# A 64-byte pad ahead of the weight ring's second pool: matmul operands at one address modulo 512

## Chip, cores and metric

One core of one Trainium2 chip. The metric is the device time of one execution in microseconds (us); the kernel before was run three times. SBUF, the core's working memory, has 128 partitions, and an address below is a byte offset in a partition. The engines are named as in the profile: PE is TensorE's matmuls, PEld its weight loads, DVE VectorE, ACT ScalarE, POOL GpSimd, SP SyncE.

## What is computed

A two-layer encoder trunk over 256 frames of width 2048, in fp32. Layer 0 mixes with RWKV-7 and Mamba-2 heads behind one input projection, layer 1 with chunked attention; each ends with a SwiGLU block. What matters here is that nearly all work is eight dense products of a 256-row activation with a large weight:

```python
p = h @ w_in                                          # layer 0: 2048 -> 6144 (padded)
y = jnp.concatenate([y_a, y_b], axis=-1) @ w_out      # 2048 -> 2048
f = (jax.nn.silu(h @ w_gate) * (h @ w_up)) @ w_down   # both layers: 2048 -> 2 x 5632 -> 2048
q, k, v = jnp.split(h @ w_qkv, 3, axis=-1)            # layer 1: 2048 -> 6144
out = attention(q, k, v) @ w_out                      # 2048 -> 2048
```

## The kernel before

**The products.** Each weight is cut into blocks of 128 rows by 512 columns. `stream` (L218) brings two blocks with one 512 KB DMA into a `raw` buffer (four of them) and splits each into two fp32r tiles: ACT copies `raw` to `hi` (L235), DVE writes the remainder to `lo` (L236). The activation is split in the same way into a high and a low part (`sh` and `sl`, in the feed-forward's second product `hh` and `hl`, in attention's output product `oh` and `ol`). `mm_chunk` (L240) then makes one 512-column chunk of the output from 16 weight blocks (44 in the feed-forward's second product), and issues for each block six matmuls: for both halves t of the 256 rows,

```python
pe.matmul(o, lhsT=xh, rhs=h_[:, :width], ...)   # L255  high x hi
pe.matmul(o, lhsT=xh, rhs=l_[:, :width], ...)   # L256  high x lo
pe.matmul(o, lhsT=xl, rhs=h_[:, :width], ...)   # L257  low x hi
```

The **stationary** operand (`lhsT`) is a 128x128 slice of the activation, loaded into the array ahead of its matmul; the **moving** operand (`rhs`) is the weight tile, 512 columns that are streamed past it. Below, "a block" is one weight block and its six matmuls, from one L255 with t = 0 to the next.

**The order.** In the program's order the products are w_in (192 blocks), w_oab (64), then w_gu (352: gate and up) and w_dn (176) of layer 0, w_qkv (192), w_oc (64), and w_gu (352) and w_dn (176) of layer 1. Among their matmuls stand the rest of PE's work, in plain fp32: transposes against an identity matrix in `cc`, attention's scores and values, the two recurrences of layer 0. The feed-forward transposes its hidden tile `sg` (`ht`, L376) as soon as DVE has made it (L367); attention transposes each head's probabilities (`pt`, L905) behind a softmax on DVE and ACT.

**Where the tiles lie.** Pools lie one behind another in SBUF, in the order in which they are opened. `cst` holds constants, `cc` among them; `wpool` the `raw` buffers and five `hi` and five `lo` tiles; `S` the activations of 4 KB (`sh` and `sl` of every product but w_dn and w_oc); `sm` small statistics. Behind `sm` come first the pools of layer 0's mixer (R, R1, R2, M). When that mixer is done they are given up, and in their place open `wx` (L848), with four more `hi` and four more `lo` tiles, and behind it in turn the pools of the feed-forward (`sg`, `hh`, `hl`) and of attention (`oh`, `ol` among them).

From then on `stream` takes its tiles from a ring of nine turns:

```python
ring[:] = [wpool, wx, wpool, wx, wpool, wx, wpool, wx, wpool]     # L849
wp = ring[turn[0] % len(ring)]; turn[0] += 1                      # L230, once a block
```

The turn counter has run since the first block of w_in, so the pool of each block can be worked out: block 5 of chunk 9 of layer 0's w_gu has turn 192 + 64 + 9 x 16 + 5 = 405, a multiple of nine, so that it and the block ahead of it (turn 404, remainder 8) both lie in `wpool`. In w_in all blocks lie in `wpool`.

The addresses at which the built program puts the operands of the products, modulo 512:

```
operand                                          pool     address mod 512
moving, from wpool (all of w_in, 5 turns of 9)   wpool    192
moving, from wx (4 turns of 9)                   wx       128
stationary of w_in, w_oab, w_gu, w_qkv           S        192
stationary of w_dn (hh, hl), w_oc (oh, ol)       ff, O    128
```

A stationary slice starts a multiple of 512 bytes into its tile, so these remainders hold for all slices.

Of the kernel before, what the change touches and what calls it, by code (L numbers as in the profile page):

```python
# [9 lines left out]
F32 = mybir.dt.float32  # L10
# [6 lines left out]
P = 128  # L17
# [124 lines left out]
def encoder_body(ctx: ExitStack, tc: tile.TileContext, A):  # L142
# [7 lines left out]
    turn = [0]  # L150
    S = ctx.enter_context(tc.tile_pool(name="S", bufs=12))
    sm = ctx.enter_context(tc.tile_pool(name="sm", bufs=2))
    pmm = ctx.enter_context(tc.tile_pool(name="pmm", bufs=4, space=PSUM))
    pra = ctx.enter_context(tc.tile_pool(name="pra", bufs=2, space=PSUM))
    psa = ctx.enter_context(tc.tile_pool(name="psa", bufs=2, space=PSUM))
# [790 lines left out]
```

## Time and profile before

| | |
|---|---|
| three runs, median (lowest to highest) | 2434.82 us (2432.24 to 2435.89) |
| the profiled execution: its own time, its span | 2435.0 us, 2433.2 us |
| PE busy, PEld busy | 2400.9 us (99%), 1937.6 us (80%) |
| DVE busy, ACT busy, POOL busy | 1425.6 us (59%), 1267.9 us (52%), 33.2 us (1%) |
[...]
| HBM traffic | 425 MB read, 176 GB/s over the span |

The span runs from the first to the last instruction. [...]

### The profile page before, as it was taken

To read this page: it belongs to the slowest core of one execution; us is meant where nothing else is said; L and a number is where in the kernel's file an instruction comes from. 1 tells how busy PE (TensorE), PEld (TensorE's weight loads), DVE (VectorE), ACT (ScalarE), POOL (GpSimd) and SP (SyncE) were. 2 spreads that over 40 slices of the span, in tenths; PEclk is the share of its full clock that TensorE was granted. 3 is DMA by queue.
4 is the path that set the end of the run, shared out by engine and by line. 5 is a ranking of instruction groups with operands and counts; after the bars stand their busy time and mean duration, and the time that the engine had idled before them with its cause. 6 is when DMAs were issued, how large, how long until landed. Compare 5 with 4: busy or idle time off the path is not lost.

```text
span 2433.2 us, 31534 instructions
## 1 busy us (share of the span) xinstructions
PE 2400.9 (99%) x11374; PEld 1937.6 (80%) x11374; DVE 1425.6 (59%) x2364; ACT 1267.9 (52%) x2256; POOL 33.2 (1%) x60
## 2 busy tenths in 40 slices
PE   8999999999999999999999999999999999999998
PEld 7777778778888888888887878787888888888887
DVE  5865967665555555555556555556555555555554
ACT  6646545656444444444446555556544544444443
POOL 0000000000000000000000000000000000000000
PEclk9999989999999999999999999999999999999999
DMA  6433424656666666666665655566666666666664
GB/s 228 142 110 116 136 86 130 205 175 198 185 184 187 189 183 188 185 189 194 195 206 175 181 175 161 169 188 177 190 188 183 189 182 189 185 187 189 198 194 144
DMA packets 119357, 429.17 MB, mean 176 GB/s; under 512 B 13408, under 2 KB 13664, under 8 KB 119200
## 3 DMA queue, kind: packets, MB, share of 16 engines
q1 hardware_dynamic: 115424, 415.46, 56.1%
q0 software_dynamic: 2400, 9.18, 1.4%
q10 hardware_dynamic: 1376, 2.52, 0.3%
q8 instruction: 89, 1.46, 0.2%
q14 instruction: 68, 0.56, 0.1%
HBM read 425.01 MB, written 2.10 MB: 176 GB/s over the span
## 4 chain that ended last, share of the span: by engine, by line
PE 93%; DVE 3%; ACT 1%; DMA 1%; issue 1%; SPq 0%; POOL 0%; DVEq 0%; ACTq 0%; POOLq 0%
PE mm_w_gu L256 13%; PE mm_w_gu L255 13%; PE mm_w_gu L257 13%; PE mm_w_dn L255 7%; PE mm_w_dn L257 7%; PE mm_w_dn L256 7%; PE mm_w_qkv L255 4%; PE mm_w_qkv L256 4%; PE mm_w_qkv L257 4%; PE mm_w_in L257 3%; PE mm_w_in L256 2%; PE mm_w_in L255 2%; PE mm_w_oc L255 1%; PE mm_w_oab L256 1%; PE mm_w_oc L257 1%; PE mm_w_oab L255 1%
## 5 line engine op out<-in xcount | busy, mean ns | idle before, releaser
L236 DVE TENSOR_TENSOR lo_w_gu<-raw_w_gu,hi_w_gu 128x512 fp32r<-128x512 f32 x704 | 486.3, 692 | 434.2 <-ACT hi_w_gu L235 432.8
L235 ACT CAST hi_w_gu<-raw_w_gu 128x512 fp32r<-128x512 f32 x704 | 436.3, 621 | 474.8 <-PE mm_w_gu L257 420.4
L256 PE MATMUL mm_w_gu<-lo_w_gu,sh_f 128*128 128x512 f32 x1408 | 556.6, 396 | 0.0
L255 PE MATMUL mm_w_gu<-hi_w_gu,sh_f 128*128 128x512 f32 x1408 | 555.4, 394 | 0.6 <-ACT sh_f L294 0.5
L257 PE MATMUL mm_w_gu<-hi_w_gu,sl_f 128*128 128x512 f32 x1408 | 551.6, 392 | 0.0
L236 DVE TENSOR_TENSOR lo_w_dn<-raw_w_dn,hi_w_dn 128x512 fp32r<-128x512 f32 x352 | 243.1, 692 | 230.1 <-ACT hi_w_dn L235 230.1
L235 ACT CAST hi_w_dn<-raw_w_dn 128x512 fp32r<-128x512 f32 x352 | 217.8, 620 | 258.5 <-PE mm_w_dn L257 213.7
L255 PEld LDWEIGHTS mm_w_gu<-hi_w_gu,sh_f 128*128 128x128 f32 x1408 | 263.9, 187 | 65.4 <-ACT sh_f L294 3.4
L257 PEld LDWEIGHTS mm_w_gu<-hi_w_gu,sl_f 128*128 128x128 f32 x1408 | 264.2, 188 | 60.8 <-DVE sl_f L295 1.2
L256 PEld LDWEIGHTS mm_w_gu<-lo_w_gu,sh_f 128*128 128x128 f32 x1408 | 264.0, 188 | 58.0 <-DVE lo_w_gu L236 0.3
L255 PE MATMUL mm_w_dn<-hi_w_dn,hh 128*128 128x512 f32 x704 | 278.8, 396 | 0.0
L257 PE MATMUL mm_w_dn<-hi_w_dn,hl 128*128 128x512 f32 x704 | 277.0, 394 | 0.0
L256 PE MATMUL mm_w_dn<-lo_w_dn,hh 128*128 128x512 f32 x704 | 275.3, 391 | 0.0
L236 DVE TENSOR_TENSOR lo_w_qkv<-raw_w_qkv,hi_w_qkv 128x512 fp32r<-128x512 f32 x192 | 132.3, 691 | 101.1 <-ACT hi_w_qkv L235 101.1
L235 ACT CAST hi_w_qkv<-raw_w_qkv 128x512 fp32r<-128x512 f32 x192 | 118.6, 619 | 105.2 <-PE mm_w_qkv L257 94.2
L236 DVE TENSOR_TENSOR lo_w_in<-raw_w_in,hi_w_in 128x512 fp32r<-128x512 f32 x184 | 124.8, 688 | 56.3 <-ACT hi_w_in L235 54.9
L257 PEld LDWEIGHTS mm_w_dn<-hi_w_dn,hl 128*128 128x128 f32 x704 | 132.3, 188 | 31.6
L256 PEld LDWEIGHTS mm_w_dn<-lo_w_dn,hh 128*128 128x128 f32 x704 | 132.3, 188 | 30.4
L255 PE MATMUL mm_w_in<-hi_w_in,sh_in 128*128 128x512 f32 (+1 forms) x384 | 154.6, 403 | 1.4 <-ACT hi_w_in L235 1.4
L256 PE MATMUL mm_w_qkv<-lo_w_qkv,sh_qkv 128*128 128x512 f32 x384 | 155.5, 405 | 0.0
L257 PE MATMUL mm_w_in<-hi_w_in,sl_in 128*128 128x512 f32 (+1 forms) x384 | 155.4, 405 | 0.0
L255 PEld LDWEIGHTS mm_w_dn<-hi_w_dn,hh 128*128 128x128 f32 x704 | 132.0, 188 | 28.7
(343 smaller groups left out, 2854.5 us busy)
## 6 DMA issues: line engine op xcount, KB each, us to landing
raw_w_gu<-in_w_gu SPq DMA_DIRECT2D x352, 512.0 KB, 3.6
raw_w_dn<-in_w_dn SPq DMA_DIRECT2D x176, 512.0 KB, 4.1
raw_w_qkv<-in_w_qkv SPq DMA_DIRECT2D x96, 512.0 KB, 3.6
raw_w_in<-in_w_in SPq DMA_DIRECT2D x92, 512.0 KB, 3.6
raw_w_oab<-in_w_oab SPq DMA_DIRECT2D x32, 512.0 KB, 4.3
raw_w_oc<-in_w_oc SPq DMA_DIRECT2D x32, 512.0 KB, 3.9
bias<-in_bias POOLq DMA_DIRECT2D x4, 768.0 KB, 7.4
x_in<-in_x SPq DMA_DIRECT2D x4, 512.0 KB, 10.4
```

What stands on the lines that cost most here:

```text
L235: act.copy(hi, raw[:, h, :])
L236: dve.tensor_tensor(lo, raw[:, h, :], hi.bitcast(F32), op=ALU.subtract)
L255: pe.matmul(o, lhsT=xh, rhs=h_[:, :width], start=k_ == 0, stop=False)
L256: pe.matmul(o, lhsT=xh, rhs=l_[:, :width], start=False, stop=False)
L257: pe.matmul(o, lhsT=xl, rhs=h_[:, :width], start=False, stop=k_ == nk - 1)
```

## The change

A tile of 16 floats, 64 bytes in each partition, is allocated in `sm` and used by nothing:

```diff
     sm = ctx.enter_context(tc.tile_pool(name="sm", bufs=2))
+
+    pad_sm = sm.tile([P, 16], F32, tag="pad", name="pad_sm", bufs=1)
     pmm = ctx.enter_context(tc.tile_pool(name="pmm", bufs=4, space=PSUM))
```

In the built program every address behind it is 64 bytes higher, and each engine has the same instructions in the same order with the same waits. `cst`, `wpool` and `S` lie ahead of `sm` and stay. Some start addresses, before and after:

```
                              before            after
wpool hi, first tile          38080 (192)       38080 (192)      in brackets: mod 512
S, first tile                 58560 (192)       58560 (192)
wx hi, first tile            112768 (128)      112832 (192)
sg, first tile               129152 (128)      129216 (192)
hh, first tile               137344 (128)      137408 (192)
oh, first tile               186496 (128)      186560 (192)
cc                            16512 (128)       16512 (128)
```

Modulo 2048 the `wpool` tiles stand at 1216 in both kernels, those of `wx` at 128 before and 192 after.

## Rows read from the trace of the kernel before

**Rows 1.** The page: span, and busy us of each engine (share) xinstructions.
```profile
span 2433.2 us, 31534 instructions
PE 2400.9 (99%) x11374; PEld 1937.6 (80%) x11374; DVE 1425.6 (59%) x2364; ACT 1267.9 (52%) x2256; POOL 33.2 (1%) x60
```
**Rows 2.** The page: the chain that ended last, by engine.
```profile
PE 93%; DVE 3%; ACT 1%; DMA 1%; issue 1%; SPq 0%; POOL 0%; DVEq 0%; ACTq 0%; POOLq 0%
```
**Rows 3.** Groups of PE by line and shape: count | busy us, mean ns | idle us before.
```profile
L255 PE MATMUL mm_w_gu<-hi_w_gu,sh_f 128*128 128x512 f32 x1408 | 555.4, 394 | 0.6 <-ACT sh_f L294 0.5
...
L376 PE MATMUL ht<-cc,sg 128*128 128x128 f32 x176 | 26.6, 273 | 0.0
...
L305 PE MATMUL pn_f<-cc,m_o 128*128 128x128 f32 x32 | 4.8, 272 | 0.0
```
**Rows 4.** Timeline of PE in w_in: start us, duration us, engine, line, tiles.
```profile
231.88 0.39 PE L255 MATMUL mm_w_in<-hi_w_in,sh_in 128*128 128x512 f32 x1
...
250.70 0.39 PE L257 MATMUL mm_w_in<-hi_w_in,sl_in 128*128 128x512 f32 x1
```
**Rows 5.** Timeline of PE in w_gu: first matmul of some blocks.
```profile
733.26 0.39 PE L255 MATMUL mm_w_gu<-hi_w_gu,sh_f 128*128 128x512 f32 x1
...
742.96 0.39 PE L255 MATMUL mm_w_gu<-hi_w_gu,sh_f 128*128 128x512 f32 x1
...
744.36 0.39 PE L255 MATMUL mm_w_gu<-hi_w_gu,sh_f 128*128 128x512 f32 x1
...
745.74 0.39 PE L255 MATMUL mm_w_gu<-hi_w_gu,sh_f 128*128 128x512 f32 x1
...
747.10 0.39 PE L255 MATMUL mm_w_gu<-hi_w_gu,sh_f 128*128 128x512 f32 x1
```
**Rows 6.** Timeline of PE in w_dn: first matmul of some blocks.
```profile
1101.40 0.39 PE L255 MATMUL mm_w_dn<-hi_w_dn,hh 128*128 128x512 f32 x1
...
1112.48 0.40 PE L255 MATMUL mm_w_dn<-hi_w_dn,hh 128*128 128x512 f32 x1
...
1113.87 0.39 PE L255 MATMUL mm_w_dn<-hi_w_dn,hh 128*128 128x512 f32 x1
...
1115.24 0.40 PE L255 MATMUL mm_w_dn<-hi_w_dn,hh 128*128 128x512 f32 x1
...
1116.63 0.40 PE L255 MATMUL mm_w_dn<-hi_w_dn,hh 128*128 128x512 f32 x1
```
**Rows 7.** Stretches: us, busy PE, PEld, DVE, ACT, POOL, clock, DMA share, GB/s.
```profile
231.88:250.70 18.82, 18.82 (x85) 15.58 (x83) 14.24 (x23) 17.41 (x29) 0.17 (x1) 1.00 0.52 153
733.26:758.22 24.96, 24.96 (x109) 20.24 (x108) 12.47 (x19) 12.46 (x20) 0.00 (x0) 1.00 0.64 190
1101.40:1126.34 24.94, 24.94 (x110) 20.28 (x109) 12.47 (x19) 11.16 (x18) 0.00 (x0) 1.00 0.65 209
```
**Rows 8.** Timeline of PE in w_in, behind transposes of the mixer.
```profile
125.92 0.40 PE L256 MATMUL mm_w_in<-lo_w_in,sh_in 128*128 128x512 f32 x1
...
128.69 0.39 PE L256 MATMUL mm_w_in<-lo_w_in,sh_in 128*128 128x512 f32 x1
```
**Rows 9.** Timeline of PE in attention: a head's transposes, the matmul ahead of each.
```profile
1348.89 0.40 PE L255 MATMUL mm_w_qkv<-hi_w_qkv,sh_qkv 128*128 128x512 f32 x1
1349.21 0.61 PE L905 MATMUL pt<-cc,s 128*128 128x128 f32 x3
...
1354.25 0.40 PE L255 MATMUL mm_w_qkv<-hi_w_qkv,sh_qkv 128*128 128x512 f32 x1
1354.53 0.61 PE L905 MATMUL pt<-cc,s 128*128 128x128 f32 x3
```
**Rows 10.** What reads tile sg: who ended the idle time (us, times).
```profile
  DVE sg L367: 8.9, 44
```
**Rows 11.** Lines 235 and 236: duration ns min/median/max, first and last start us.
```profile
L235 ACT CAST hi_w_gu<-raw_w_gu x704: 602/621/642, 518.6 to 2168.3; 128x512 fp32r<-128x512 f32 x176
L236 DVE TENSOR_TENSOR lo_w_gu<-raw_w_gu,hi_w_gu x704: 671/693/695, 519.2 to 2169.0; 128x512 fp32r<-128x512 f32 x176
```

## The prediction

> **What bounds the kernel now.** I read the page's list of engines first: PE is busy 2400.9 of 2433.2 us, DVE 1425.6 and ACT 1267.9 [rows 1]. The chain of waits says the same of the end: 93% of it is PE [rows 2]. So the time is the number of matmuls times the pace at which they follow each other, and anything that changes the pace by one per cent moves the end by one per cent. The groups of PE [rows 3] give the counts: 1408 L255 matmuls in w_gu are two (one for each half t) of each of 704 blocks, as the program has it. All products together have 1568 blocks of six matmuls, 9408 in all.
>
> The pace is in the timelines, from start to start. In the stretch of w_in [rows 4] 84 matmuls stand without a break; the last begins 250.70 - 231.88 = 18.82 us after the first, over 83 steps, which is 0.2267 us a step and **1.360 us for a block of six**. Here moving and stationary operands both lie at 192 modulo 512. In w_gu [rows 5] the ring shows. The block from 742.96 has its weights in `wx`, at 128, against a stationary 192, and takes 1.40 us. The next, from 744.36, is back in `wpool`, 192 against 192, and takes 1.38. The one from 745.74 is the second `wpool` block in a row (turn 405), and takes 1.36 (to 747.10), the pace of w_in. The shape and the engine's clock are the same in all three. What differs is where the weights lie, and where those of the block before lay. A whole cycle of nine blocks, from 733.26 to 745.74, takes 12.48 us: 1.387 a block. In w_dn [rows 6], where the stationary lies at 128, the cycle from 1101.40 to 1113.87 takes 12.47 us, 1.386 a block; its blocks take 1.39 (from 1112.48, `wpool` after `wx`), 1.37 (from 1113.87, second `wpool` block) and 1.39 (from 1115.24, `wx`, 128 against 128).
>
> Could another load than the addresses make w_in faster? The stretches [rows 7] show the full clock, 1.00, in all three. DMA moves 153 GB/s in that of w_in and 190 and 209 in the others, which would be a candidate; but the fast block of w_gu stands in the midst of the heavier traffic and has the same 1.36.
>
> **The change part by part.** The tile itself costs nothing: no instruction writes or reads it, and no order or wait changes. What moves is every address behind `sm`.
>
> *w_gu, w_qkv, w_oab* (704 + 192 + 64 = 960 blocks). Four blocks of nine move from 128 to 192, so that all have the pairing 192 against 192 and none follows another. I take the pace of w_in: 1.387 - 1.360 = 0.0267 us a block, 25.6 us. The bounds: nothing gained where a block stays at 1.40 and 1.38; 25.6 where all settle.
>
> *w_dn, w_oc* (352 + 64 = 416 blocks). Here the stationary moves from 128 to 192 too, and the pairing becomes the same one. From 1.3855 (12.47 / 9) to 1.360 is 0.0255 us a block, 10.6 us. The trace never shows these stationary pools (`ff`, `O`) at 192; the nearest rows are those of `S` at 192, which I take, with 0 as the other end.
>
> *w_in* (192 blocks) stays: its operands lie ahead of the pad. Together 36.2 us, if every block had the settled pace.
>
> *Breaks.* Behind other PE work the stream needs about ten steps to settle, at equal addresses too: behind transposes in w_in twelve steps take 128.69 - 125.92 = 2.77 us instead of 12 x 0.2267 = 2.72 [rows 8], which is 0.05 lost. Outside w_in some 100 such breaks stand in the program (44 groups of `ht`, 44 in attention, the rest in the norms), many with fewer steps behind them. I count 0.03 us each, between 0 (a break with nothing to settle) and the row's 0.05: 3.0 us are not gained, with 0 and 5 as ends.
>
> *Waits that now come later.* In attention a head's transposes `pt` already wait for the softmax: the matmul ahead starts 0.32 and 0.28 us before them, instead of 0.23 [rows 9], and from one to the next pass 5.32 us, a time that DVE and ACT set. PE has some 20 matmuls of the product between (5.32 us less about 0.9 for the head's own small ones, at 0.23) and gains 20 x 0.0045 = 0.09 us there, which turns into waiting. Twelve of the sixteen heads follow another one closely: 1.1 us lost. The weight loads of `ht` wait for DVE 44 times, 8.9 us in all [rows 10], in the shadow of the matmul that still runs. PE comes there some five matmuls after the one that released DVE, so at most 5 x 0.0045 = 0.02 us earlier: between 0 and 1.0 us lost, and I take 0.5.
>
> *The weights' supply* holds. A block costs ACT 0.62 and DVE 0.69 us [rows 11] of now 1.36, and the DVE group's narrow spread (671 to 695 ns, over `lo` tiles at 192 and at 128) speaks against a price of the address there. The *transposes* lose the equality with `cc` at 128 that `ht` has now; `pn_f`, whose tile at 192 is unequal to it, takes 272 ns against 273 [rows 3], so I take nothing, with 176 x 1 ns = 0.2 us as the other end.
>
> The sum: 36.2 - 3.0 - 1.1 - 0.5 = 31.6 us. Against the profiled execution's own 2435.0 us that is 2403.4; it stands 0.2 above the median of the three runs, so that I forecast **2403 us**.
>
> [...]
>
> **The rivals.**
>
> *Only part of it counts (2423 us).* The rule could be one of equality modulo 2048, not 512: `wpool` stands at 1216 there, `wx` at 192 after the change. Then the `wx` blocks keep their 1.40 and only the four `wpool` blocks behind them go from 1.38 to 1.36: 4 x 0.02 = 0.08 of a cycle's 12.48 us, times 1376 / 9 = 153 cycles, 12 us. Against it: stationary slices step by 512 bytes through all four remainders modulo 2048, and the 84 matmuls in w_in [rows 4] keep one pace through all of them.
>
> *No change (2435 us).* The slow blocks may be slow since the ring alternates between two far pools, or for where `wx` lies, whatever the remainder. For it: in the trace before, `wx` and 128 always go together in w_gu. Against it: in w_dn, in the same ring, `wx` and `wpool` blocks both take 1.39, so that it isn't the pool alone.
>
> *Slower (2455 us).* Equal addresses may be the bad case and w_in an exception. For it: in w_dn the block at equal addresses, 128 against 128, takes 1.39 and the unequal one from 1113.87 takes 1.37. If every block came to the 1.40 that the slowest ones take, 960 x 0.013 + 416 x 0.0145 = 18.5 us would be added, nearly 2454, with the waits behind it 2455. It decides where a run of equal blocks settles: above 1.387 us the kernel is slower, below it faster. Against it: such runs are what w_in is made of, and they settle at 1.360; the 128 block in w_dn always follows one at 192 and is never settled.
>
> *More than counted (2398 us):* no breaks and waits lost, the full 36.2.
>
> **How the numbers follow.** The forecast has 0.84, since the pairing that it leads to stands in the trace at its pace, under the same clock and the same traffic. "More" has 0.02, "part" 0.06, "no change" 0.05, "slower" 0.03. What a measurement of this kernel can tell from no change is about 0.2%, 5 us: faster 0.84 + 0.02 + 0.06 = 0.92, same 0.05, slower 0.03. The range goes down to 2395, which is the full 36.2 with the 3 us by which the shown runs scatter. Upward it goes to 2412: 9 us above the forecast, about what w_dn and w_oc bring, should they stay as they are. That covers the first and the last of the cases and leaves some 0.15 outside.
>
> **What would show it.** In the changed kernel's timeline each block of w_gu, w_dn, w_qkv and w_oc, `wx` or `wpool`, should take 1.36 us, but for some ten matmuls behind each break, and a cycle of nine 12.24. PE's busy time should fall by about 32 us and its share stay at 99%; w_in's timeline, ACT's 0.62 and DVE's 0.69 should stay. `pt` should start some 0.4 us behind the matmul ahead. Blocks of 1.40 in the places of `wx`, alternating with 1.36, would prove "part" right; 1.40, 1.38 and 1.36 in the old order "no change"; 1.387 or more throughout the last rival. A w_dn that settles elsewhere than w_gu would mean that the stationary pool counts by itself.

## The result and the profile after

Four runs of the changed kernel took 2402.06 us in the median (2400.69 to 2404.57), beside 2433.74 us of the kernel before: a ratio of 0.987, 95% interval 0.9853 to 0.9887. The forecast was 2403 us.

The page of the changed kernel, span, PE and chain, to be held against [rows 1, 2]:

```profile
span 2399.9 us, 31534 instructions
PE 2367.5 (99%) x11374; PEld 1937.3 (81%) x11374; DVE 1424.7 (59%) x2364; ACT 1271.0 (53%) x2256; POOL 33.2 (1%) x60
...
PE 93%; DVE 4%; ACT 1%; issue 1%; DMA 1%; POOL 0%; SPq 0%; DVEq 0%; ACTq 0%; POOLq 0%
```

PE is busy 33.4 us less, as the span is 33.3 us shorter, and the other engines are busy as before, at a mean granted clock of 0.994 before and 0.992 after: the same work, at a quicker pace of PE alone. In the profile a matmul lasts some 0.39 us while the next starts 0.227 us behind it, so the pace is read from the starts. It stands in the timeline of PE, here the first matmuls of blocks in w_gu and in w_dn, each pair of rows nine blocks apart (L257 is the line that was L255 before):

```profile
728.14 0.39 PE L257 MATMUL mm_w_gu<-hi_w_gu,sh_f 128*128 128x512 f32 x1
...
740.38 0.39 PE L257 MATMUL mm_w_gu<-hi_w_gu,sh_f 128*128 128x512 f32 x1
...
1090.00 0.39 PE L257 MATMUL mm_w_dn<-hi_w_dn,hh 128*128 128x512 f32 x1
...
1102.24 0.39 PE L257 MATMUL mm_w_dn<-hi_w_dn,hh 128*128 128x512 f32 x1
```

740.38 - 728.14 and 1102.24 - 1090.00 are both 12.24 us, 1.360 a block, where the cycles took 12.48 and 12.47 [rows 5, 6]. Four of the nine blocks lie in `wx`, and the pace goes through them without a trace of the ring.

Where the 33 us came from is read from the first and last starts of L255's matmuls in each product. The kernel before:

```profile
L255 PE MATMUL mm_w_gu<-hi_w_gu,sh_f x1408: 387/394/508, 530.6 to 2179.9; 128*128 128x512 f32 x176
L255 PE MATMUL mm_w_dn<-hi_w_dn,hh x704: 389/396/481, 1032.6 to 2424.7; 128*128 128x512 f32 x176
L255 PE MATMUL mm_w_in<-hi_w_in,sh_in x384: 366/389/795, 13.8 to 438.9; 128*128 128x512 f32 x176, 128*128 128x464 f32 x16
L255 PE MATMUL mm_w_qkv<-hi_w_qkv,sh_qkv x384: 387/394/525, 1278.5 to 1585.2; 128*128 128x512 f32 x192
L255 PE MATMUL mm_w_oc<-hi_w_oc,oh x128: 393/396/475, 1585.9 to 1677.9; 128*128 128x512 f32 x128
L255 PE MATMUL mm_w_oab<-hi_w_oab,yah x64: 388/394/395, 439.6 to 517.7; 128*128 128x512 f32 x64
```

and the changed one, where the same line is L257:

```profile
L257 PE MATMUL mm_w_gu<-hi_w_gu,sh_f x1408: 388/389/500, 527.4 to 2151.1; 128*128 128x512 f32 x176
L257 PE MATMUL mm_w_dn<-hi_w_dn,hh x704: 388/389/476, 1021.0 to 2391.4; 128*128 128x512 f32 x176
L257 PE MATMUL mm_w_in<-hi_w_in,sh_in x384: 368/389/795, 13.2 to 437.0; 128*128 128x512 f32 x176, 128*128 128x464 f32 x16
L257 PE MATMUL mm_w_qkv<-hi_w_qkv,sh_qkv x384: 387/389/500, 1262.6 to 1566.2; 128*128 128x512 f32 x192
L257 PE MATMUL mm_w_oc<-hi_w_oc,oh x128: 388/389/475, 1566.9 to 1657.4; 128*128 128x512 f32 x128
L257 PE MATMUL mm_w_oab<-hi_w_oab,yah x64: 389/389/389, 437.7 to 514.6; 128*128 128x512 f32 x64
```

From each product's first start to that of the next:

| stretch | before, us | after, us | gained |
|---|---|---|---|
| up to w_in's first matmul | 13.8 | 13.2 | 0.6 |
| w_in | 425.8 | 424.5 | 1.3 |
| w_oab | 91.0 | 89.7 | 1.3 |
| w_gu, layer 0 | 502.0 | 493.6 | 8.4 |
| w_dn, layer 0 | 245.9 | 241.6 | 4.3 |
| w_qkv | 307.4 | 304.3 | 3.1 |
| w_oc, and w_gu of layer 1 to its last start | 594.0 | 584.2 | 9.8 |
| from there to w_dn's last start | 244.8 | 240.3 | 4.5 |
| the end | 8.5 | 8.5 | 0 |

The products behind w_in gained 31.4 us; the rest, 1.9, lies ahead of them, where the pad moves no operand of a product and where w_in's stage scatters by more than that from run to run (below). The medians differ by 31.7.

### The profile page after: what moved, and what is told of

The parts are those of the page before. It is cut to its first block, busy times and chain, and to the rows that moved or that the text cites. A ratio compares the mean times of both kernels' runs of the same rounds, so it can differ in the third digit from the quotient of the medians.

```text
span 2399.9 us, 31534 instructions
## 1 busy us (share of the span) xinstructions
PE 2367.5 (99%) x11374; PEld 1937.3 (81%) x11374; DVE 1424.7 (59%) x2364; ACT 1271.0 (53%) x2256; POOL 33.2 (1%) x60
## 4 chain that ended last, share of the span: by engine, by line
PE 93%; DVE 4%; ACT 1%; issue 1%; DMA 1%; POOL 0%; SPq 0%; DVEq 0%; ACTq 0%; POOLq 0%
PE mm_w_gu L257 13%; PE mm_w_gu L259 13%; PE mm_w_gu L258 13%; PE mm_w_dn L257 7%; PE mm_w_dn L258 7%; PE mm_w_dn L259 7%; PE mm_w_qkv L257 4%; PE mm_w_qkv L258 4%; PE mm_w_qkv L259 4%; PE mm_w_in L259 3%; PE mm_w_in L258 2%; PE mm_w_in L257 2%; PE mm_w_oc L258 1%; PE mm_w_oc L257 1%; PE mm_w_oc L259 1%; DVE lo_w_in L238 1%
## 5 line engine op out<-in xcount | busy, mean ns | idle before, releaser
L257 PE MATMUL mm_w_gu<-hi_w_gu,sh_f 128*128 128x512 f32 x1408 | 550.9, 391 | 0.7 <-ACT sh_f L296 0.5
L258 PE MATMUL mm_w_gu<-lo_w_gu,sh_f 128*128 128x512 f32 x1408 | 550.0, 391 | 0.0
L259 PE MATMUL mm_w_gu<-hi_w_gu,sl_f 128*128 128x512 f32 x1408 | 548.7, 390 | 0.0
L257 PEld LDWEIGHTS mm_w_gu<-hi_w_gu,sh_f 128*128 128x128 f32 x1408 | 264.3, 188 | 57.3 <-ACT sh_f L296 3.4
L259 PEld LDWEIGHTS mm_w_gu<-hi_w_gu,sl_f 128*128 128x128 f32 x1408 | 264.4, 188 | 55.5 <-DVE sl_f L297 1.2
L258 PEld LDWEIGHTS mm_w_gu<-lo_w_gu,sh_f 128*128 128x128 f32 x1408 | 264.4, 188 | 53.3 <-DVE lo_w_gu L238 0.3
L258 PE MATMUL mm_w_dn<-lo_w_dn,hh 128*128 128x512 f32 x704 | 274.1, 389 | 0.0
L257 PE MATMUL mm_w_dn<-hi_w_dn,hh 128*128 128x512 f32 x704 | 274.1, 389 | 0.0
L259 PE MATMUL mm_w_dn<-hi_w_dn,hl 128*128 128x512 f32 x704 | 274.0, 389 | 0.0
L257 PE MATMUL mm_w_in<-hi_w_in,sh_in 128*128 128x512 f32 (+1 forms) x384 | 154.1, 401 | 1.4 <-ACT hi_w_in L237 1.4
L259 PE MATMUL mm_w_in<-hi_w_in,sl_in 128*128 128x512 f32 (+1 forms) x384 | 155.0, 404 | 0.0
L258 PE MATMUL mm_w_qkv<-lo_w_qkv,sh_qkv 128*128 128x512 f32 x384 | 154.2, 402 | 0.0
L259 PEld LDWEIGHTS mm_w_dn<-hi_w_dn,hl 128*128 128x128 f32 x704 | 132.1, 188 | 27.3
L258 PEld LDWEIGHTS mm_w_dn<-lo_w_dn,hh 128*128 128x128 f32 x704 | 132.1, 188 | 27.3
L257 PEld LDWEIGHTS mm_w_dn<-hi_w_dn,hh 128*128 128x128 f32 x704 | 132.1, 188 | 27.3
```

What stands on the lines that cost most here:

```text
L257: pe.matmul(o, lhsT=xh, rhs=h_[:, :width], start=k_ == 0, stop=False)
L258: pe.matmul(o, lhsT=xh, rhs=l_[:, :width], start=False, stop=False)
L259: pe.matmul(o, lhsT=xl, rhs=h_[:, :width], start=False, stop=k_ == nk - 1)
```

## The experiments

All are edits of the changed kernel, by more unused tiles and, in two of them, by where an operand begins in its tile or pool. "Difference" is the address of the stationary operand less that of the moving one.

**same_place_elsewhere**: the remainder, or the difference?

```diff
+    front = ctx.enter_context(tc.tile_pool(name="front", bufs=1))
+    front.tile([P, 16], F32, tag="pad", name="pad_front")
     wpool = ctx.enter_context(tc.tile_pool(name="wpool", bufs=5))
```

> The changed kernel with 64 bytes more ahead of the first weight pool: every operand of the products moves from 192 to 256 modulo 512, so all stay equal to each other at another remainder. Theory 1 (only the difference between the stationary and the moving address counts): the settled block of six stays at 1.360 us everywhere and the time at 2402 us, within 3. Theory 2 (the remainder 192 itself is the good one): blocks leave 1.360 in all products, w_in too; at the 1.387 of the kernel before that is 1568 x 0.027 = 42 us more, 2444.

Measured: 2404.53 us (2402.48 to 2406.57), ratio 0.9871, interval 0.9855 to 0.9888. All eight products settle at 226.67 ns from start to start (the mean over steps of the timeline that begin at least 14 matmuls behind a break; so below). The profiled span is 4.9 us longer than that of the changed kernel, and all of it is in w_in's stage, 429.4 us here, whose code and settled pace are the same; its mean granted clock is 0.95 against 0.96. In the profiles of this case that stage takes 423.9 to 429.4 us, so below the paces are compared, and not the times of single runs. Theory 2 is out: 192 is nothing special.

**shift_a, shift_b, shift_c**: the stationary tiles of three products moved against moving tiles that all stay at 192, so that nothing alternates. The edit, with shift_a's numbers:

```diff
+            shift = mx.enter_context(tc.tile_pool(name=f"shift{l}", bufs=1, reuse_waits="tile"))
+            shift.tile([P, (64, 128)[l] // 4], F32, tag="shift", name=f"shift_{l}")
             hp = mx.enter_context(tc.tile_pool(name=f"ff{l}", bufs=2 * NFF, reuse_waits="tile"))
...
+            shift = mx.enter_context(tc.tile_pool(name="shift_o", bufs=1, reuse_waits="tile"))
+            shift.tile([P, 192 // 4], F32, tag="shift", name="shift_o")
             O = mx.enter_context(tc.tile_pool(name="O", bufs=8, reuse_waits="tile"))
```

> The changed kernel with the stationary tiles alone moved in three products, the moving ones all staying at 192: in w_dn of layer 0 the stationary stands 64 bytes above the moving operand modulo 512, in w_dn of layer 1 128 above, in w_oc 192 above. Theory 1 (the difference counts): the blocks of w_dn of layer 0 settle at 6 x 233.3 = 1.40 us, what the wx blocks of w_gu showed before at the same difference; the other two show new values, which this run is for; w_gu, w_qkv and w_in stay at 1.360. Rival (the alternation of two moving addresses made the blocks slow, not the difference): nothing alternates here, so all three products stay at 1.360 and the time at 2402 us. By theory 1 w_dn of layer 0 alone costs 176 x 0.04 = 7 us.

> The same with other differences: w_dn of layer 0 256 above, w_dn of layer 1 320 above, w_oc 384 above. Theory 1 (the difference counts, modulo 512): other values than 1.360 in each; were the rule one modulo 256, w_dn of layer 0 would stay at 1.360. Rival (only alternation counts): 1.360 in all three, 2402 us.

> The same with w_dn of layer 0 448 above (64 below), w_dn of layer 1 32 above, w_oc 96 above. Theory 1: w_dn of layer 0 settles at what the wpool blocks of w_dn showed before at the same difference, 232 + 226 + 229 ns twice, 1.374 us a block; 32 above shows whether the optimum at 0 is flat (1.360) or sharp (up to 1.40). Rival (only alternation counts): 1.360 in all three, 2402 us.

Measured, one run each: 2420.08, 2414.39 and 2413.61 us. The timeline of w_dn of layer 0 in shift_a (difference 64), six blocks apart:

```profile
1046.14 0.39 PE L257 MATMUL mm_w_dn<-hi_w_dn,hh 128*128 128x512 f32 x1
...
1054.54 0.39 PE L257 MATMUL mm_w_dn<-hi_w_dn,hh 128*128 128x512 f32 x1
```

and in shift_b (difference 256):

```profile
1046.07 0.39 PE L257 MATMUL mm_w_dn<-hi_w_dn,hh 128*128 128x512 f32 x1
...
1054.23 0.39 PE L257 MATMUL mm_w_dn<-hi_w_dn,hh 128*128 128x512 f32 x1
```

8.40 us and 8.16 us: 1.400 and 1.360 a block. With nothing alternating, a difference of 64 is as slow as the `wx` blocks were [rows 5], so that alternation alone is out as the cause; and 256 is as good as 0, against what I had taken for the modulus. The pairs 64 and 320 (both 233.3 ns), 128 and 384 (both 232.4) and 192 and 448 (both 228.9) say the same: **in these runs the difference counts modulo 256.** In shift_c 448 gives 1.373 us a block, as expected, and 32 gives 1.400, against 1.360 at 0: upward the optimum is narrower than 32 bytes.

**ring_256_apart**: the ring alternates again, by 256.

```diff
+        gap = ctx.enter_context(tc.tile_pool(name="gap", bufs=1, reuse_waits="tile"))
+        gap.tile([P, 256 // 4], F32, tag="gap", name="gap")
         wx = ctx.enter_context(tc.tile_pool(name="wx", bufs=4, reuse_waits="tile"))
```

> The changed kernel with 256 bytes more ahead of the pool wx, so that the ring alternates again between two remainders modulo 512 (192 and 448), and the stationary tiles of w_dn and w_oc stand at 448. The run before, in which a stationary 256 above the moving operand kept 1.360 us, brought theory 1b: the difference counts modulo 256. Theory 1b: every block settles at 1.360 and the time is that of the changed kernel, 2402 us within 3. Theory 1 (modulo 512, as I had it): the wx blocks of w_gu, w_qkv and w_oab and the wpool blocks of w_dn leave 1.360, and the time goes back by half or more of the gain, to 2418 to 2434. Rival (two alternating remainders cost by themselves): about 2434.

Measured: 2405.81 us (2402.62 to 2406.57), ratio 0.9872, interval 0.9855 to 0.9888. Timeline of w_gu, the first matmuls of a `wx` block, the `wpool` block behind it, a second `wpool` block, and the next:

```profile
740.11 0.39 PE L257 MATMUL mm_w_gu<-hi_w_gu,sh_f 128*128 128x512 f32 x1
...
741.47 0.39 PE L257 MATMUL mm_w_gu<-hi_w_gu,sh_f 128*128 128x512 f32 x1
...
742.83 0.39 PE L257 MATMUL mm_w_gu<-hi_w_gu,sh_f 128*128 128x512 f32 x1
...
744.19 0.39 PE L257 MATMUL mm_w_gu<-hi_w_gu,sh_f 128*128 128x512 f32 x1
```

1.36, 1.36 and 1.36, where the same three blocks took 1.40, 1.38 and 1.36 before [rows 5]. The alternation by itself cost nothing here; only its remainder modulo 256 did.

**shift_d**: finer steps. The edit is that of shift_a with 224, 160 and 224, and in attention the operand begins 16 bytes into its tile:

```diff
-                sh = O.tile([P, 4, T], F32R, tag="o", name=f"oh{g}")
-                sl = O.tile([P, 4, T], F32R, tag="o", name=f"ol{g}")
+                sh = O.tile([P, 4 * T + 64], F32R, tag="o", name=f"oh{g}")[:, 4:4 * T + 4].rearrange("p (q t) -> p q t", t=T)
+                sl = O.tile([P, 4 * T + 64], F32R, tag="o", name=f"ol{g}")[:, 4:4 * T + 4].rearrange("p (q t) -> p q t", t=T)
```

> The changed kernel with the stationary tiles moved against the moving ones (all at 192): w_dn of layer 0 by 224 (32 below modulo 256), w_dn of layer 1 by 160, w_oc by 240 (16 below). The values so far, in ns a matmul: 0 gives 226.7, 32 and 64 give 233.3, 96 gives 234.3, 128 gives 232.4, 192 gives 228.9. Theory 1b: a curve that falls from 96 over 128 and 192 to 0 and jumps up behind it; then 160 lies between 232.4 and 228.9, 224 between 228.9 and 226.7 (1.373 to 1.360 us a block), 240 at about 226.7 or below. A block under 1.355 us at 224 or 240 would show that equality is not the best place, and a kernel with all products there would beat the changed one.

Measured, one run: 2415.16 us. No smooth curve: 160 and 224 both give 233.3 ns, above 192 between them; 240 gives 226.7. The expectation of a falling curve was wrong. All values together, by difference modulo 256:

```
difference, bytes   0      16     32     64     96     128    160    192    224    240
ns a matmul       226.7  226.7  233.3  233.3  234.3  232.4  233.3  228.9  233.3  226.7
```

Nothing tried is better than equality, whose pace of 226.7 ns holds for 16 bytes to either side and is gone at 32 (233.3). So no version came out of the scan that beats the changed kernel.

**split_high_low**: does a matmul pay for its own stationary operand, or for the one that is loaded beside it?

```diff
+                if j == 0 and l == 1:
+                    hp.tile([P, 16], F32, tag="pad_h", name="pad_h", bufs=1)
-                sh = hp.tile([P, 4, T], F32R, tag="hid", name=f"hh_{l}_{j}")
-                sl = hp.tile([P, 4, T], F32R, tag="hid", name=f"hl_{l}_{j}")
+                sh = hp.tile([P, 4, T], F32R, tag="hid", name=f"hh_{l}_{j}", bufs=NFF)
+                if j == 0:
+                    hp.tile([P, (16, 48)[l]], F32, tag="pad_l", name="pad_l", bufs=1)
+                sl = hp.tile([P, 4, T], F32R, tag="hid_l", name=f"hl_{l}_{j}", bufs=NFF)
```

In w_oc the 16-byte edit of shift_d, without its pool.

> The changed kernel with only one half of the stationary tiles moved. In w_dn of layer 0 the low part hl stands 64 above the moving operand and the high part hh is equal to it; in layer 1 hh stands 64 above and hl is equal; in w_oc both stand 16 above. Theory 3 (a matmul pays for its own pairing): of the three matmuls of a half block, in layer 0 only L259's step is longer (233.3 against 226.7: 1.373 us a block), in layer 1 L257's and L258's (1.387). Theory 4 (a matmul pays for the weight load that runs beside it, which is that of the next matmul): in layer 0 the step of L258 is the longer one, beside which hl is loaded, in layer 1 those of L259 and L257; the blocks are the same 1.373 and 1.387. If the steps settle only over several matmuls, as behind breaks, the place of the long step is not to be read, and only the sum is. w_oc at 16 above: 1.360 if the optimum has some width upward, 1.400 if it jumps within 16 bytes.

Measured, one run: 2414.41 us. Layer 0, where `hl` alone stands off, in the timeline of w_dn:

```profile
1060.19 0.39 PE L257 MATMUL mm_w_dn<-hi_w_dn,hh 128*128 128x512 f32 x1
1060.42 0.39 PE L258 MATMUL mm_w_dn<-lo_w_dn,hh 128*128 128x512 f32 x1
1060.65 0.40 PE L259 MATMUL mm_w_dn<-hi_w_dn,hl 128*128 128x512 f32 x1
1060.89 0.39 PE L257 MATMUL mm_w_dn<-hi_w_dn,hh 128*128 128x512 f32 x1
...
1061.58 0.39 PE L257 MATMUL mm_w_dn<-hi_w_dn,hh 128*128 128x512 f32 x1
```

1.39 us for a block. The mean steps are 228.3, 229.2 and 235.8 ns (L257, L258, L259) in layer 0, and 225.9, 235.8 and 231.7 in layer 1: sums of 1.387 us a block in both. Theory 3 and theory 4 each wanted 1.373 in layer 0, and neither fits; this mixture of good and bad pairings costs two thirds of the full price (0.027 of 0.040 us a block) whether one or two of the three matmuls stand off. Which pairing a matmul pays for stays open. w_oc at 16 kept 226.7 ns.

**all_96_apart**: the worst difference everywhere. The edit of shift_a with 96 in all three places, and

```diff
+    ahead = ctx.enter_context(tc.tile_pool(name="ahead", bufs=1))
+    ahead.tile([P, 24], F32, tag="pad", name="pad_ahead")
     S = ctx.enter_context(tc.tile_pool(name="S", bufs=12))
     sm = ctx.enter_context(tc.tile_pool(name="sm", bufs=2))
 
-    pad_sm = sm.tile([P, 16], F32, tag="pad", name="pad_sm", bufs=1)
+    pad_sm = sm.tile([P, 56], F32, tag="pad", name="pad_sm", bufs=1)
```

> The changed kernel with the worst difference found, 96 bytes modulo 256, between stationary and moving operand in every product, w_in too; nothing else changes. Theory 1b (the difference modulo 256 sets the pace of the whole stream): each of the 1568 blocks settles at the 1.406 us that w_oc showed at this difference, 0.0457 more than at equality. 1376 blocks outside w_in make 62.9 us, the 192 of w_in between 4 (where its stream waits for DVE and ACT anyway) and 8.8; some 3 us less for the breaks, where nothing has settled at either difference. 2402 + 64 to 69 is 2466 to 2471; allowing for the scatter of w_in's stage 2460 to 2475, a ratio to the kernel before of 1.010 to 1.016. Rival (a pace below PE's own limit is partly hidden, or w_dn and w_oc alone are sensitive to the stationary): w_gu and w_qkv keep 1.360 to 1.39 and the time stays under 2440.

Measured: 2463.95 us (2460.94 to 2465.44), ratio 1.012, interval 1.0101 to 1.0138. Its page and, in the timeline of w_gu (L259 is the first line of a block here), two blocks nine apart:

```profile
PE 2429.7 (99%) x11374; PEld 1944.8 (79%) x11374; DVE 1426.5 (58%) x2364; ACT 1269.5 (52%) x2256; POOL 33.1 (1%) x60
```

```profile
736.78 0.39 PE L259 MATMUL mm_w_gu<-hi_w_gu,sh_f 128*128 128x512 f32 x1
...
749.43 0.40 PE L259 MATMUL mm_w_gu<-hi_w_gu,sh_f 128*128 128x512 f32 x1
```

12.65 us, 1.406 a block, and every product settles at that pace. The same instructions, 61.9 us above the changed kernel's median by nothing but the place of their operands (`wx` and `wpool` stand 256 apart here, which cost nothing in ring_256_apart, 1.36 us a block). It came 2 us under the 2466 to 2471 that I had worked out; each w_gu took 14.7 us more than at equality (508.3 against 493.6) instead of 352 x 0.0457 = 16.1. About half of the 1.4 us that are missing lies in steps close behind breaks, and most of the rest at the transposes `ht`, which wait less for DVE when PE is slower (118 ns from one to the next in the changed kernel, 109 here, in the mean).

This run also settles a rival that no experiment was made for. ACT and DVE write `hi` and `lo` tiles at the moving operand's own remainders, so that the price could come from a clash between PE's reads of the stationary operand and these writes or the DMA's. Near the end of w_dn in layer 1 all weights are there, and for 7 us nothing but PE works:

```profile
2440.30:2447.30 7.00, 7.00 (x31) 5.63 (x30) 0.00 (x0) 0.00 (x0) 0.00 (x0) 1.00 0.00 0
```

```profile
2440.33 0.40 PE L260 MATMUL mm_w_dn<-lo_w_dn,hh 128*128 128x512 f32 x1
...
2447.12 0.39 PE L259 MATMUL mm_w_dn<-hi_w_dn,hh 128*128 128x512 f32 x1
```

The 29 steps from the first to the last of these rows take 6.79 us, 234 ns each, the full price; in the same stretch of the changed kernel (2381.5 to 2388.2 us, as idle) the steps are 226.7 ns in the mean. So the price came here with no other engine and no DMA at work.

**all_32_up**: all operands 32 bytes higher, equal to each other. The edit is that of same_place_elsewhere with 8 floats.

> The changed kernel with 32 bytes more ahead of the first weight pool, so that all operands stand at 224 modulo 512, equal to each other but at no multiple of 64. Theory 1b: 1.360 us in all products, 2402 us within 4. Rival (the place must be a multiple of 64 bytes, which all runs at 1.360 had so far for the moving operand): blocks of 1.37 to 1.40 and 15 to 60 us more.

Measured, one run: 2404.3 us, 226.7 ns in all products. At 224 modulo 512, no multiple of 64, the place itself cost nothing.

## Why the prediction was right

**The main step held.** The prediction took the pace of w_in, 1.360 us a block, for every block once all operands stand at 192, and that is what each product shows. Its ground was that a fast block in w_gu [rows 5] shared everything with the slow ones but the addresses; all_96_apart and the shifts show that this was the cause, since they bring the loss back, in sizes that the settled pace accounts for, with no other change.

**The terms.** Settled blocks would have given 36.2 us, and 31.4 arrived against a sum of 31.6. For w_oab, w_gu, w_qkv and w_oc the forecast is 25.6 + 1.6 less the 4.6 of breaks and waits, 22.6, and the table gives 1.3 + 8.4 + 3.1 + 9.8 = 22.6; for w_dn, 352 x 0.0255 = 9.0, it gives 8.8. That the sum came within 0.2 us is in part luck: two small waits were mis-sized, in opposite directions. *Waits that now come later* came out smaller at `pt`. In attention the matmul ahead of `pt` now starts 0.38 us earlier than `pt`:

```profile
1326.88 0.39 PE L257 MATMUL mm_w_qkv<-hi_w_qkv,sh_qkv 128*128 128x512 f32 x1
1327.26 0.61 PE L907 MATMUL pt<-cc,s 128*128 128x128 f32 x3
```

where it was 0.28 to 0.32 in the two heads of [rows 9], so the gain is indeed turned into waiting; but over the twelve heads the step grew from 0.329 to 0.364 us in the mean, 0.035 and not 0.09, about 0.4 us together instead of 1.1. At `ht` they came out larger. Its weight loads wait 9.8 us instead of 8.9 [rows 10]:

```profile
  DVE sg L369: 9.8, 44
```

and the running matmul no longer hides all of it. Each of the 22 hidden tiles is transposed in a group of two and a group of six. The steps ahead of both groups are 226 to 239 ns, as before, but in the group of two, whose first weight load is the one that waits for DVE longer than before, the second transpose begins later. Such a group and the matmul behind it, before and after:

```profile
852.43 0.38 PE L376 MATMUL ht<-cc,sg 128*128 128x128 f32 x2
852.57 0.48 PE L256 MATMUL mm_w_gu<-lo_w_gu,sh_f 128*128 128x512 f32 x1
```

```profile
843.90 0.44 PE L378 MATMUL ht<-cc,sg 128*128 128x128 f32 x2
844.10 0.48 PE L258 MATMUL mm_w_gu<-lo_w_gu,sh_f 128*128 128x512 f32 x1
```

The step between the two grew from 119 to 164 ns in the mean, 1.0 us over the 22: the upper end of the prediction's bounds, and not 0.5. *Breaks* were sized about right. The 8143 steps from one product matmul to the next outside w_in sum to 1897.65 us before and 1864.51 after, 33.1 gained, where the settled pace would give 36.2 x 8143 / 8256 = 35.7: 2.6 us were not gained there, against 3.0. What is left, 36.2 - 31.4 - 2.6 - 0.4 - 1.0 = 0.8, lies in the steps into and among PE's other work. The *transposes* cost nothing, as taken: inside the groups of six the steps of `ht` are 109 ns before and after. The prediction's ground for it, 272 against 273 ns [rows 3], compared durations, which do not give a pace: the 273 ns of a transpose stand beside starts 109 ns apart.

**The rivals.** "Part" fell with the changed kernel itself: its `wx` blocks stand at 192 modulo 2048, those of `wpool` at 1216, and all take 1.36. Its price of 12 us was not consistent either: were the `wx` blocks still slow, the `wpool` blocks behind them would have kept the 1.38 that the prediction itself put down to the block before. "No change" fell with it too, since the changed kernel alternates between the same two pools; ring_256_apart adds that two remainders may alternate at no cost. "Slower" rested on the 1.39 of the block at 128 against 128 [rows 6]; where every neighbour is equal modulo 256 as well, blocks of w_dn at 448 against 448 (ring_256_apart) and 192 against 192 (the changed kernel) settle at 1.36, so that the 1.39 came from the unequal blocks around it, as the prediction supposed.

**Where it was too narrow.** The whole text speaks of equality modulo 512, which the runs do not bear out: a difference of 256 is as good as none (1.360 us a block in shift_b, as at equality). Nothing in the trace before could tell, as it holds only 0, 64 and -64. The forecast did not hang on it.

By the runs the difference of the two addresses is worth up to 7.6 ns a matmul (226.7 at equality to 234.3 at 96 bytes). Why it counts, and whether loading the stationary operand and reading the moving one hinder each other, is not shown: no run here took one of them away.

## What to carry to other kernels

Where PE streams without a pause, look at the steps between the starts of like matmuls, block by block: here a pace that followed the ring of buffers (1.40, 1.38 and 1.36 us a block) with no wait anywhere came from the buffers' addresses. In such a case place the pools so that weights and activations of one product begin at the same address modulo 256; here that took 64 bytes and was worth 1.3%, and the span between the best and the worst placing of the same instructions was 2.5% (ratios of 0.987 and 1.012 to the kernel before). Only one form was tried: fp32r, a stationary operand of 128x128 loaded anew for each matmul, a moving one of 128x512. A small unused tile ahead of a pool moved this kernel by that much, so small differences between two versions that also shift addresses should not be put down to the edit one had in mind.

## What was not expected of the hardware

The curve over the difference is not smooth: 226.7 ns within 16 bytes of equality, 233.3 at 32, a lower 228.9 at 192 with 233.3 to either side.

In two short stretches of w_in at a granted clock of 0.50 (255.5 to 257.0 us before, and 168.0 to 169.9 in all_96_apart) the price is not seen. There matmuls of the kernel before, at equal addresses, start

```profile
255.77 0.63 PE L257 MATMUL mm_w_in<-hi_w_in,sl_in 128*128 128x512 f32 x1
256.20 0.63 PE L255 MATMUL mm_w_in<-hi_w_in,sh_in 128*128 128x512 f32 x1
256.62 0.63 PE L256 MATMUL mm_w_in<-lo_w_in,sh_in 128*128 128x512 f32 x1
```

0.43 and 0.42 us apart, and those of all_96_apart, at the worst difference, start

```profile
168.54 0.63 PE L259 MATMUL mm_w_in<-hi_w_in,sh_in 128*128 128x512 f32 x1
168.97 0.63 PE L260 MATMUL mm_w_in<-lo_w_in,sh_in 128*128 128x512 f32 x1
169.39 0.63 PE L261 MATMUL mm_w_in<-hi_w_in,sl_in 128*128 128x512 f32 x1
```

just as far. These are a few steps only. Half the granted clock did not double the step: 0.42 to 0.43 us is less than twice the settled 226.7 ns at 1.00 (453.4), and than twice the 234.3 of the worst difference (468.6). What sets the step at either clock, these runs do not show.
